# The first modulation stage: weight blocks stationary, conditioning columns moving

## The chip, the core and the metric

The kernel is one program on one core of a Trainium2 chip. The core has a matrix engine (TensorE; PE for its matmuls, PEld for the loads of the operand that stays in the array), a vector engine (DVE), a scalar engine (ACT), a general engine (POOL), and a queue from which nearly all transfers are issued (SP). Each engine takes its instructions in order; they meet through semaphores. The metric is device time in microseconds of one execution, and each kernel is run several times.

A matmul has two operands. The stationary one is loaded into the array first, in an instruction of its own, and then the columns of the moving one are streamed past it. A matmul of 32-bit floats is executed as two passes, so that each matmul of the program shows in the trace as two loads and two matmuls. Where the program splits a number itself into a high and a low part ("fp32r"), one pass is made for each.

## What is computed

One layer of a diffusion backbone on 1024 latent tokens and 256 context tokens, with a model width of 1024. What matters here is its first step: both conditioning vectors go through one matrix, and the first two of the six results modulate the normalised inputs.

```python
m_lat = (jax.nn.silu(c) @ w_mod[l] + b_mod[l]).reshape(B_, 1, N_MOD, D)
m_ctx = (jax.nn.silu(c_ctx) @ w_mod[l] + b_mod[l]).reshape(N_MOD, D)
h_lat = rms_norm(x, norm_mix[l]) * (1.0 + m_lat[:, :, 1]) + m_lat[:, :, 0]
h_ctx = rms_norm(ctx, norm_mix[l]) * (1.0 + m_ctx[1]) + m_ctx[0]
...
ccq, ccf, ccb, cci, ... = features(h_ctx, w_in[l], ...)
aq, ak, av, bq, bk, bv, cq, cf, cb, ci, cg, gates = features(h_lat, w_in[l], ...)
```

After it come the projections of the context tokens, the projections of the latent tokens, a recurrence, two attentions, a merge, and a gated feed-forward part, which fill the rest of the time.

## The kernel before

Channels lie on the 128 partitions, in KT = 8 blocks of 128. The host lays out the part of the matrix that the first step needs as eight blocks `w_mod01[i]` of 1 MB: 128 partitions (input channel within its block) by 2 results (shift and scale, index j) by 8 input blocks (k) by 128 output channels. `scc` holds the two activated conditioning vectors, 128 by 8 by 2.

The stage is the loop `for i in range(KT)` near the start of `build`. It runs on four engines, and for PE its order is the order of the code (`manual_schedule`); on the other engines and the SP queue a scheduler orders the instructions, and every transfer waits until the transfer eight before it has landed. For six of the eight blocks the two columns `scc[:, k]` are the stationary operand and the weights stream: eight matmuls of 256 columns into `pr`, two rows of results. ACT copies the two rows out (`row`), and two small transposes per block (`mod_row`, into `pm`) bring the channels back onto the partitions; the transposes of a block stand in the PE queue behind the matmuls of the next one. The other two blocks (1 and 4, `MOD_OFF`) are worked off by DVE in 16 operations each into `acc`, and PE transposes the sums (`pt`), which DVE adds up. `mod_done` adds the bias and makes the scale `a01`.

Along the way come the norm of the context (`ctx_norm`: a square on ACT, a sum on DVE, two transposes `rcc` on PE, a power on POOL, two transposes `rpc`), and for each finished block `ctx_h`: a product on DVE (`cx`) and a bias on ACT, which make the block k of the context's input `ch`. The constants of the recurrence (`lower_bounds`, tile `lbs`) and three weight blocks for the context projections (`w_raw`) are loaded between the weight blocks.

Behind the stage two generators are woven together: `ctx_all`, the projections of the context (PE matmuls `czf`, `czb`, `czv` for four heads, then `ckv`), and `lat_norm`, which squares the latent tokens on ACT (`sqx` from `xn`), turns their norm on PE (`rpx`), and makes the latent tokens' input `hh`, `hl` with `finish_h`. When both are done the first projection of the latent tokens, `zq`, begins.

Of the kernel before, what the change touches and what calls it, by code (L numbers as in the profile page):

```python
# [9 lines left out]
F32 = mybir.dt.float32  # L10
# [3 lines left out]
ALU = mybir.AluOpType  # L14
AX = mybir.AxisListType
# [3 lines left out]
P = 128  # L19
D = 1024  # L20
KT = D // P
# [22 lines left out]
WPRIO_C = 30  # L44
WM = 8
WPRIO_D = 30
WAT = 5
MPRIO = 100
CXAT = 1
LBAT = 3  # L50
NORMAT = 3

MOD_OFF = (1, 4)
MOD_FIN = {3: (1,), 6: (4,)}
CTX_K = (0, 2, 1, 3, 5, 4, 6, 7)

NPOOL = 6
# [13 lines left out]
U_C = {"q": 0, "f": 4, "b": 8, "v": 12, "g": 16, "gate": 20}  # L71
# [20 lines left out]
def build(tc, ins, out, dbg=None):  # L92
    nc = tc.nc
    V, A, G, T, SP = nc.vector, nc.scalar, nc.gpsimd, nc.tensor, nc.sync
    with ExitStack() as top:
# [12 lines left out]
        def ct(shape, name, dt=F32):  # L108
            return const.tile(shape, dt, tag=name, name=name)

        def cs(shape, name, dt=F32):
            return small.tile(shape, dt, tag=name, name=name)
# [7 lines left out]
        def bank(tag, name, shape=(P, 4, P), dt=F32):  # L120
            return ps.tile(list(shape), dt, tag=tag, name=name)
# [12 lines left out]
        scc = cs([P, KT, 2], "scc")  # L134
# [5 lines left out]
        ident = ct([P, P], "ident")  # L140
# [40 lines left out]
        def w_raw(src, nk, ncol):  # L181

            tag, bufs = (("wr", WR), ("wh", WH), ("wl", WL))[cnt[0] % 3]
            cnt[0] += 1
            with tc.high_priority(offset=wprio[0]):
                raw = wp.tile([P, 1024], F32, tag=tag, name=f"{tag}{cnt[0]}", bufs=bufs)
                SP.dma_start(raw, src)
            return raw.rearrange("p (k n) -> p k n", k=nk)
# [24 lines left out]
        def lower_bounds():  # L213

            SP.dma_start(lbr, ins["lb"])
            V.tensor_tensor(out=lt, in0=lbr, in1=lbr, op=ALU.subtract)
            A.activation(lt, lt, AF.Exp)
            V.reciprocal(lb, lt)
            V.tensor_tensor(out=lt, in0=lt, in1=lb, op=ALU.mult)
            V.tensor_tensor(out=lt, in0=lt, in1=lt, op=ALU.subtract)  # L220
            V.tensor_scalar(out=lb, in0=lt, scalar1=0.0, scalar2=1.0, op0=ALU.max, op1=ALU.min)
            V.tensor_scalar(out=oml, in0=lb, scalar1=-1.0, scalar2=1.0, op0=ALU.mult, op1=ALU.add)
# [40 lines left out]
        def rms_bc(r, n, name, tag):  # L263
            nt = n // P
            if n > 512:
                rp = mm2(f"rp{name}").rearrange("p a b -> p (a b)")
            else:
                rp = bank(tag, f"rp{name}", (P, n))
            for t in range(nt):
                T.transpose(rp[:, t * P:(t + 1) * P], r[:, t:t + 1].to_broadcast([P, P]), ident)  # L270
            return rp[:, :n]
# [7 lines left out]
        with ExitStack() as s0:  # L279
# [7 lines left out]
            xm_ = Aligned(xw.enter_context(tc.tile_pool(name="xm_", bufs=1)))  # L287

            units0 = []
            accs = {}  # L290
            pend = []
            rows = []

            def mod_done(i, pm):

                V.tensor_tensor(out=m01[:, i], in0=pm, op=ALU.add,
                                in1=bmod[:, i:i + KT + 1:KT][:, :, None].to_broadcast([P, 2, 2]))
                V.scalar_tensor_tensor(out=a01[:, i], in0=m01[:, i, 1], scalar=1.0,
                                       in1=gains[:, 0, i:i + 1].to_broadcast([P, 2]), op0=ALU.add, op1=ALU.mult)
                pend.append(i)  # L300

            def mod_row(i, row):
                pm = bank("a", f"pm{i}", (P, 2, 2))
                for j in range(2):
                    T.transpose(pm[:, j], row[:, j], ident[0:2, 0:2])
                mod_done(i, pm)

            def ctx_norm():
                csq = xm_.tile([P, KT, LC], F32, tag="csq", name="csq")
                A.activation(csq, cx, AF.Square)  # L310
                css = xm_.tile([P, LC], F32, tag="css", name="css")
                V.reduce_sum(out=css, in_=csq.rearrange("p k t -> p t k"), axis=AX.X)
                return rms_r(xm_, [css], LC, "c", False)

            def ctx_h():
                while pend:
                    k = pend.pop(0)
                    V.scalar_tensor_tensor(out=cx[:, k], in0=cx[:, k], scalar=a01[:, k, 1:2], in1=rc,
                                           op0=ALU.mult, op1=ALU.mult)
                    A.activation(ch[:, k], cx[:, k], AF.Identity, bias=m01[:, k, 0, 1:2])  # L320

            mo = ExitStack()
            mo.enter_context(tc.manual_schedule(engines={mybir.EngineType.PE}))
            for i in range(KT):
                wm = xm_.tile([P, 2, KT, P], F32, tag="wm", name=f"wm{i}", bufs=WM)
                SP.dma_start(wm, ins["w_mod01"][i].rearrange("p (j k c) -> p j k c", j=2, k=KT))
                if i == LBAT:
                    lower_bounds()
                if i == CXAT:
                    SP.dma_start(cx, ins["ctxT"].rearrange("(k p) t -> p k t", p=P))  # L330
                if WAT <= i < WAT + 3:
                    units0.append(w_raw(ins["w_cm"][U_C["fbv"[i - WAT]]], KT, P))
                if i in MOD_OFF:
                    acc = accs[i] = xm_.tile([P, 2, 2, P], F32, tag="acc", name=f"acc{i}", bufs=2)
                    for k in range(KT):
                        for v in range(2):
                            if k == 0:
                                V.tensor_scalar(out=acc[:, v], in0=wm[:, :, k], scalar1=scc[:, k, v:v + 1], scalar2=None,
                                                op0=ALU.mult)
                            else:  # L340
                                V.scalar_tensor_tensor(out=acc[:, v], in0=wm[:, :, k], scalar=scc[:, k, v:v + 1],
                                                       in1=acc[:, v], op0=ALU.mult, op1=ALU.add)
                    continue
                pr = bank("b", f"pr{i}", (P, 2, P))
                with tc.high_priority(offset=MPRIO):
                    for k in range(KT):
                        T.matmul(pr[0:2], scc[:, k], wm[:, :, k], start=k == 0, stop=k == KT - 1)
                    row = xm_.tile([2, 2, P], F32, tag="row", name=f"row{i}", bufs=3)
                    A.copy(row, pr[0:2])
                rows.append((i, row))  # L350
                if len(rows) > 1:
                    mod_row(*rows.pop(0))
                if i == KT - 1:
                    mod_row(*rows.pop(0))
                for n in MOD_FIN.get(i, ()):
                    pm = xm_.tile([P, 2, 2], F32, tag="pm", name=f"pm{n}")
                    pt = bank("b", f"pt{n}", (P, 2, 2, P))
                    for v in range(2):
                        for j in range(2):
                            T.transpose(pt[:, j, v], accs[n][:, v, j], ident)  # L360
                    V.reduce_sum(out=pm, in_=pt, axis=AX.X)
                    mod_done(n, pm)
                if i == NORMAT:
                    rc = ctx_norm()
                if i == NORMAT + 2:
                    rc = rms_bc(rc, LC, "c", "b")
                if i >= NORMAT + 2:
                    ctx_h()
# [125 lines left out]
            for h in range(CH):  # L494
                pt = bank("a", f"ckp{h}", (P, 2, 2, P))
# [75 lines left out]
        with ExitStack() as sp3:  # L571
# [5 lines left out]
            for nm, g in (("A", None), ("q", qnb), ("k", knb)):  # L577
                tb = p3.tile([P, LT, 2, 2, 32], F32, tag=f"tb{nm}", name=f"tb{nm}", bufs=1)
                for r in range(2):
                    if g is None:  # L580
                        G.tensor_copy(tb[:, :, :, r], cs)
                    else:
                        G.tensor_tensor(out=tb[:, :, :, r], in0=cs,
                                        in1=g[:, None, None, r * 32:(r + 1) * 32].to_broadcast([P, LT, 2, 32]),
# [199 lines left out]
        for k in range(KQ):  # L784
            h1, h2 = xm[k], xm[k + KQ]
            b = {nm: [p[:, k] for p in blk[nm]] for nm in ("T1", "T2", "T3")}
# [171 lines left out]
        for tb in range(2):  # L958
            xt = p2.tile([P, KT, LH], F32, tag="xt", name=f"xt{tb}", bufs=2)
            ss = []  # L960
            for mh in range(2):
# [7 lines left out]
                for f2_ in range(FT // 2):  # L969
                    w = w_unit(ins["w_down"][mh * (FT // 2) + f2_], 2, 512)  # L970
                    for f1 in range(2):
                        f = f2_ * 2 + f1
# [21 lines left out]
        for i in range(4, KT):  # L994
            z0 = 0
            for n in LAST if i == KT - 1 else (LH,):
                z = (bank("b", f"dl{i}{z0}", (P, LH)) if (i + (z0 > 0)) % 2 else mm2(f"dl{i}{z0}")[:, 0])[:, :n]
                for f0 in range(0, FT, 8):
                    nk = min(8, FT - f0)
                    w = w_unit(ins["w_dlast"][i - 4][:, f0 * P:(f0 + nk) * P], nk, P)  # L1000
                    for k in range(nk):
                        f = f0 + k
# [574 lines left out]
```

## Time and profile before

| | |
|---|---|
| time, median of 3 runs | 2128.88 us |
| lowest and highest | 2126.53 and 2129.55 us |
| span of the profiled execution, first to last instruction | 2127.9 us |
| PE busy | 2085.8 us, 98% |
| DVE busy | 1380.5 us, 65% |
| ACT busy | 1001.2 us, 47% |
| POOL busy | 288.1 us, 14% |
| transfers, mean over the span | 108 GB/s |

The profiled execution's time is known as its span; no other time is listed for it. It lies 1.0 us below the median and inside the range of the runs.

In a row of the timeline stand the start of an instruction or of a run of alike ones, how long it lasted, the engine, the line of the program, the operation, and out<-in with the shapes; "x16" is the number of instructions in the run; in brackets stand the idle time of the engine before it and what ended that. A shape "128*2 128x256" of a matmul says that the stationary operand has 128 rows and 2 columns and that 256 columns stream. A matmul is shown with its way through the array, so that matmuls overlap in the rows; the pace is read from one start to the next. A row of windows gives for each stretch the busy time and number of instructions of each engine, the granted TensorE clock as a share of full speed, the busy share of the transfer engines, and GB/s.

### The profile page before, as it was taken

The page shows a single profiled execution, that of the slowest core. Times are in us where ns is not written, and L with a number is a line of the kernel's source. Part 1 is how long each engine was busy: PE and PEld are TensorE (multiplying, and loading weights), DVE is VectorE, ACT ScalarE, POOL GpSimd, SP SyncE. Part 2 cuts the span into 40 slices and gives each one's busy share as a digit, 9 for nine tenths or more (in the row PEclk, how much of TensorE's full clock was granted, in tenths as well). Part 3 has the DMA queues.
Part 4 walks back from the last instruction along what each step waited for, and adds up shares of the span by engine and source line. Part 5 has one row for each costly group of instructions (what it writes and reads, how often), then busy time and mean ns, then how long its engine had stood idle before and what let it go on. Part 6 is the DMA issues. An engine that isn't in the chain of part 4 may idle for free.

```text
span 2127.9 us, 30555 instructions
## 1 busy us (share of the span) xinstructions
PE 2085.8 (98%) x11686; PEld 1743.1 (82%) x11686; DVE 1380.5 (65%) x2299; ACT 1001.2 (47%) x1761; POOL 288.1 (14%) x257
## 2 busy tenths in 40 slices
PE   7999999999999999999999999999999999999997
PEld 4888888888988888878888788888888888888887
DVE  4736756636665777678887746569777777664423
ACT  4333333311123777678888734346445544453222
POOL 0000000010021222100000000011333344100111
PEclk9999999999999999999999999999999999999999
DMA  9511111136543211211100354641222222285342
GB/s 359 207 44 36 46 50 41 46 113 214 186 137 123 78 59 41 80 55 35 35 28 28 115 200 142 194 156 55 99 79 89 80 80 88 81 287 201 109 126 86
DMA packets 95490, 229.28 MB, mean 108 GB/s; under 512 B 10736, under 2 KB 35824, under 8 KB 94320
## 3 DMA queue, kind: packets, MB, share of 16 engines
q1 hardware_dynamic: 95344, 227.33, 32.1%
q8 instruction: 92, 1.51, 0.3%
q14 instruction: 54, 0.44, 0.1%
HBM read 181.68 MB, written 45.61 MB: 107 GB/s over the span
## 4 chain that ended last, share of the span: by engine, by line
PE 69%; DVE 3%; ACT 2%; issue 1%; DMA 1%; POOL 1%; SPq 0%; DVEq 0%; ACTq 0%; POOLq 0%
PE pp L1321 4%; PE gz L199 3%; PE dn L929 3%; PE dn L928 3%; PE dn L930 3%; PE gz L200 3%; PE gz L201 3%; PE up L852 2%; PE up L853 2%; PE up L854 2%; PE po L1307 2%; PE po L1308 2%; PE br L200 2%; PE br L201 2%; PE br L199 2%; PE upd L853 2%
## 5 line engine op out<-in xcount | busy, mean ns | idle before, releaser
L175 ACT CAST wh<-wr 128x1024 fp32r<-128x1024 f32 (+1 forms) x139 | 145.1, 1044 | 398.7 <-PE dn L929 69.1
L176 DVE TENSOR_TENSOR wl<-wr,wh 128x1024 fp32r<-128x1024 f32 (+1 forms) x139 | 171.1, 1232 | 221.1 <-ACT wh L175 206.7
L1326 DVE TENSOR_TENSOR pl<-pp,ph 128x512 fp32r<-128x512 f32 x236 | 159.3, 687 | 29.2 <-ACT ph L1325 23.5
L199 PE MATMUL gz<-hh,wh 128*128 128x512 f32 x384 | 156.3, 408 | 3.1 <-ACT gs L523 3.1
L1325 ACT CAST ph<-pp 128x512 fp32r<-128x512 f32 x236 | 135.7, 587 | 37.4 <-PE pp L1321 35.3
L201 PE MATMUL gz<-hh,wl 128*128 128x512 f32 x384 | 152.3, 397 | 0.0
L200 PE MATMUL gz<-hl,wh 128*128 128x512 f32 x384 | 152.1, 396 | 0.0
L210 PE MATMUL tm<-wl,hh 128*128 128x256 f32 x384 | 108.9, 283 | 3.3 <-DVE wl L176 3.3
L209 PE MATMUL tm<-wh,hh 128*128 128x256 f32 x384 | 108.9, 284 | 0.9 <-ACT qo L615 0.9
L211 PE MATMUL tm<-wh,hl 128*128 128x256 f32 x384 | 108.6, 283 | 0.0
L1307 PE MATMUL po<-ph,VHL 128*128 128x512 f32 x236 | 106.1, 450 | 1.4 <-ACT ph L1325 1.0
L929 PE MATMUL dn<-ac,wh 128*128 128x512 f32 x256 | 99.7, 390 | 0.0
L930 PE MATMUL dn<-ac,wl 128*128 128x512 f32 x256 | 99.6, 389 | 0.0
L928 PE MATMUL dn<-ac,wh 128*128 128x512 f32 x256 | 99.6, 390 | 0.0
L1308 PE MATMUL po<-pl,VHL 128*128 128x512 f32 x236 | 97.1, 411 | 0.1
L199 PEld LDWEIGHTS gz<-hh,wh 128*128 128x128 f32 x384 | 72.7, 189 | 17.2 <-ACT gs L523 5.2
L201 PEld LDWEIGHTS gz<-hh,wl 128*128 128x128 f32 x384 | 72.5, 189 | 15.0
L200 PEld LDWEIGHTS gz<-hl,wh 128*128 128x128 f32 x384 | 72.8, 190 | 11.6
L210 PEld LDWEIGHTS tm<-wl,hh 128*128 128x128 f32 x384 | 73.7, 192 | 4.3 <-DVE wl L176 4.0
L1321 PE MATMUL pp<-ident,plat 128*128 128x128 f32 x512 | 76.6, 273 | 0.0
L1321 PEld LDWEIGHTS pp<-ident,plat 128*128 128x128 f32 x512 | 62.7, 140 | 16.9 <-DVE pl L1326 1.2
L199 PE MATMUL br<-yh,wh 128*128 128x512 f32 x192 | 74.3, 390 | 1.6 <-ACT yh L1468 1.6
(1420 smaller groups left out, 5898.7 us busy)
## 6 DMA issues: line engine op xcount, KB each, us to landing
wr<-in_w_cm SPq DMA_DIRECT2D x48, 512.0 KB, 3.7
wr<-in_w_up SPq DMA_DIRECT2D x44, 512.0 KB, 3.5
wr<-in_w_down SPq DMA_DIRECT2D x33, 512.0 KB, 3.5
wmr<-in_w_mod SPq DMA_DIRECT2D x32, 512.0 KB, 4.5
gate_d<-gs SPq DMA_DIRECT2D x48, 256.0 KB, 2.3
sgt<-gate_d SPq DMA_DIRECT2D x24, 512.0 KB, 3.4
act_d<-u SPq DMA_DIRECT2D x22, 512.0 KB, 2.6
st<-act_d SPq DMA_DIRECT2D x44, 256.0 KB, 4.5
```

Source lines behind the costliest of these rows:

```text
L175: A.copy(hi[:, :n], raw[:, :n])
L176: (lo_eng or V).tensor_tensor(out=lo[:, :n], in0=raw[:, :n], in1=hi[:, :n].bitcast(F32), op=ALU.subtract)
L199: T.matmul(psl, wh[:, k, c], hh[:, k0 + k, cols], start=s, stop=False)
L200: T.matmul(psl, wh[:, k, c], hl[:, k0 + k, cols], start=False, stop=False)
L201: T.matmul(psl, wl[:, k, c], hh[:, k0 + k, cols], start=False, stop=e)
L210: T.matmul(psl, hh[:, k, toks], wl[:, k % 4, :], start=False, stop=False)
L928: T.matmul(z, w[0][:, c], h[0], start=s, stop=False)
L929: T.matmul(z, w[0][:, c], h[1], start=False, stop=False)
L930: T.matmul(z, w[1][:, c], h[0], start=False, stop=e)
L1307: T.matmul(po, vv, ph, start=n == 0, stop=False)
L1321: T.transpose(pp[:, h], PT(h, n), ident)
L1326: V.tensor_tensor(out=pl, in0=pp, in1=ph.bitcast(F32), op=ALU.subtract)
```

## The change

All eight weight blocks are now requested first, followed by the constants and the three weight blocks for the context. Then each of the eight blocks is worked off on PE alone, with the operands exchanged: a piece of 128 by 128 weights is stationary and the two columns of `scc` stream, so that the results come out with the channels on the partitions. The path over DVE, the copies of the rows and all the transposes back are gone.

```diff
-WAT = 5
-MPRIO = 100
-LBAT = 3
-MOD_OFF = (1, 4)
-MOD_FIN = {3: (1,), 6: (4,)}
...
+            def wm_load(i):
                 wm = xm_.tile([P, 2, KT, P], F32, tag="wm", name=f"wm{i}", bufs=WM)
                 SP.dma_start(wm, ins["w_mod01"][i].rearrange("p (j k c) -> p j k c", j=2, k=KT))
-                if i == LBAT:
-                    lower_bounds()
+                wms.append(wm)
+
+            for i in range(KT):
+                wm_load(i)
                 if i == CXAT:
                     SP.dma_start(cx, ins["ctxT"].rearrange("(k p) t -> p k t", p=P))
-                if WAT <= i < WAT + 3:
-                    units0.append(w_raw(ins["w_cm"][U_C["fbv"[i - WAT]]], KT, P))
-                if i in MOD_OFF:
...
+            lower_bounds()
+            for nm in "fbv":
+                units0.append(w_raw(ins["w_cm"][U_C[nm]], KT, P))
+            for i in range(KT):
+                wm = wms[i]
+                pm = bank("ab"[i % 2], f"pm{i}", (P, 2, 2))
+                for j in range(2):
                     for k in range(KT):
...
-                pr = bank("b", f"pr{i}", (P, 2, P))
-                with tc.high_priority(offset=MPRIO):
-                    for k in range(KT):
-                        T.matmul(pr[0:2], scc[:, k], wm[:, :, k], start=k == 0, stop=k == KT - 1)
-                    row = xm_.tile([2, 2, P], F32, tag="row", name=f"row{i}", bufs=3)
-                    A.copy(row, pr[0:2])
-                rows.append((i, row))
...
+                        T.matmul(pm[:, j], wm[:, j, k], scc[:, k], start=k == 0, stop=k == KT - 1)
+                mod_done(i, pm)
                 if i == NORMAT:
                     rc = ctx_norm()
```

How this moves the instructions is shown at three places. In these rows stand the line, the operation, out<-in with the number of the tile, the shape of the result, and how often the row repeats. First PE, in the stage from its third matmul group to the first context projection, before:

```order
L305 MATMUL pm_168<-ident,row_133 128x2 x2
L347 MATMUL pr_183<-wm_173,scc 2x256 x8
L305 MATMUL pm_194<-ident,row_166 128x2 x2
L360 MATMUL pt_200<-ident,acc_138 128x128 x4
L249 MATMUL rcc_213<-ident,css 128x128 x2
L347 MATMUL pr_242<-wm_238,scc 2x256 x8
L305 MATMUL pm_253<-ident,row_192 128x2 x2
L270 MATMUL rpc<-ident,rsc 128x128 x2
L347 MATMUL pr_273<-wm_269,scc 2x256 x8
```

And the same stretch now:

```order
L330 MATMUL pm_191<-scc,wm_127 128x2 x16
L330 MATMUL pm_210<-scc,wm_129 128x2 x16
L244 MATMUL rcc_234<-ident,css 128x128 x2
L330 MATMUL pm_240<-scc,wm_131 128x2 x16
L330 MATMUL pm_259<-scc,wm_133 128x2 x16
L265 MATMUL rpc<-ident,rsc 128x128 x2
L330 MATMUL pm_293<-scc,wm_135 128x2 x16
L330 MATMUL pm_314<-scc,wm_137 128x2 x16
L409 MATMUL czv_399<-wl_151,ch 128x128 x8
L401 MATMUL czf_354<-ch,wr_147 128x256 x8
```

A block is now 16 matmuls with a result of 2 columns, where it was 8 matmuls with a result of 256 columns and 2 transposes; the stage holds eight such blocks on PE, where it held six. Of the first head's `czv` half now stands ahead of its `czf`.

Second ACT, from the square of the context to the second head, before (`ch` is the context's input, `sqx` a square of latent tokens `xn`, `snegcf` and `cF` read the result of `czf`):

```order
L349 COPY row_251<-pr_242 2x256
L320 ACTIVATE ch<-cx,m_97 128x256 x4
L349 COPY row_282<-pr_273 2x256
L320 ACTIVATE ch<-cx,m_97 128x256 x2
L389 ACTIVATE sqx_367,rsx<-xn_365 128x1024
L349 COPY row_315<-pr_306 2x256
L389 ACTIVATE sqx_371,rsx<-xn_369 128x1024
L320 ACTIVATE ch<-cx,m_97 128x256 x2
L389 ACTIVATE sqx_389,rsx<-xn_387 128x1024
L1033 ACT_TABLE_LOAD
L1033 ACTIVATE snegcf_359<-czf_350 128x256
```

And now:

```order
L307 ACTIVATE ch<-cx,m_97 128x256 x7
L212 ACT_TABLE_LOAD
L212 ACTIVATE lbs<-lbs 128x8
L307 ACTIVATE ch<-cx,m_97 128x256
L358 ACTIVATE sqx_371,rsx<-xn_369 128x1024
L358 ACTIVATE sqx_375,rsx<-xn_373 128x1024
L1002 ACT_TABLE_LOAD
L1002 ACTIVATE snegcf_363<-czf_354 128x256
```

The copies of rows are gone; the first two squares of latent tokens have moved behind the last block of `ch`, and the third behind the first head's `czf`.

Third ACT again, further on, at the second head's projections, where the squares end. Before:

```order
L389 ACTIVATE sqx_439,rsx<-xn_437 128x1024
L1033 ACTIVATE snegcf_432<-czf_423 128x256
L1034 ACTIVATE cF<-czf_423 128x256
L389 ACTIVATE sqx_443,rsx<-xn_441 128x1024
L1033 ACTIVATE snegcb_456<-czb_447 128x256
L1034 ACTIVATE cF<-czb_447 128x256
```

And now:

```order
L1002 ACTIVATE snegcf_436<-czf_427 128x256
L1003 ACTIVATE cF<-czf_427 128x256
L358 ACTIVATE sqx_443,rsx<-xn_441 128x1024
L1002 ACTIVATE snegcb_460<-czb_451 128x256
L1003 ACTIVATE cF<-czb_451 128x256
L358 ACTIVATE sqx_447,rsx<-xn_445 128x1024
L410 COPY cV<-czv_482 128x2x128
```

The eighth and last square stood ahead of the two operations that read the second `czb` and stands behind them now. On PE the eight transposes `rpx` that need all the squares stood ahead of the second head's `czv`; now 13 of the 16 matmuls of that `czv` stand ahead of them. A few operations behind the start of `zq` the queues have the same order again in both kernels, to the end.

More of the change, by code (lines that the diff above doesn't have):

```diff
@@ L289, in build @@
             units0 = []
-            accs = {}
             pend = []
-            rows = []
             def mod_done(i, pm):
@@ L300, in mod_done @@
                 pend.append(i)
[L302 to L306, printed above, removed]
             def ctx_norm():
@@ L323, in build @@
             mo.enter_context(tc.manual_schedule(engines={mybir.EngineType.PE}))
-            for i in range(KT):
+            wms = []
+            def wm_load(i):
                 wm = xm_.tile([P, 2, KT, P], F32, tag="wm", name=f"wm{i}", bufs=WM)
                 SP.dma_start(wm, ins["w_mod01"][i].rearrange("p (j k c) -> p j k c", j=2, k=KT))
-                if i == LBAT:
-                    lower_bounds()
+                wms.append(wm)
+            for i in range(KT):
+                wm_load(i)
@@ L329, in build @@
                 if i == CXAT:
                     SP.dma_start(cx, ins["ctxT"].rearrange("(k p) t -> p k t", p=P))
-                if WAT <= i < WAT + 3:
-                    units0.append(w_raw(ins["w_cm"][U_C["fbv"[i - WAT]]], KT, P))
-                if i in MOD_OFF:
-                    acc = accs[i] = xm_.tile([P, 2, 2, P], F32, tag="acc", name=f"acc{i}", bufs=2)
-                    for k in range(KT):
[L336 to L343, printed above, removed]
@@ L344, in build @@
-                pr = bank("b", f"pr{i}", (P, 2, P))
-                with tc.high_priority(offset=MPRIO):
-                    for k in range(KT):
-                        T.matmul(pr[0:2], scc[:, k], wm[:, :, k], start=k == 0, stop=k == KT - 1)
-                    row = xm_.tile([2, 2, P], F32, tag="row", name=f"row{i}", bufs=3)
-                    A.copy(row, pr[0:2])
-                rows.append((i, row))
[L351 to L362, printed above, removed]
+            lower_bounds()
+            for nm in "fbv":
+                units0.append(w_raw(ins["w_cm"][U_C[nm]], KT, P))
```

## The prediction

> **What bounds the kernel now.** I read the page first, then the windows of the stage, then the timeline.
>
> ```profile
> PE 2085.8 (98%) x11686; PEld 1743.1 (82%) x11686; DVE 1380.5 (65%) x2299; ACT 1001.2 (47%) x1761; POOL 288.1 (14%) x257
> ```
>
> PE is busy for 98% of the span, so a time that the first stage adds to PE's queue is carried to the end unless PE waits for something later that absorbs it. The question is how long PE needs until the first context projection, and what it meets behind it.
>
> ```profile
> 30.00:40.00 10.00, 8.63 (x44) 4.58 (x42) 4.18 (x14) 5.93 (x14) 0.00 (x0) 1.00 1.04 408
> ...
> 7.80 5.44 PE L347 MATMUL pr<-wm,scc 128*2 128x256 f32 x16 [7.80 <-DMA wm<-in_w_mod]
> 15.68 3.62 PE L347 MATMUL pr<-wm,scc 128*2 128x256 f32 x16 [2.44 <-DMA wm<-in_w_mod]
> 23.68 0.38 PE L249 MATMUL rcc<-ident,css 128*128 128x128 f32 x2
> 27.75 0.43 PE L270 MATMUL rpc<-ident,rsc 128*128 128x128 f32 x2
> 33.67 3.62 PE L347 MATMUL pr<-wm,scc 128*2 128x256 f32 x16 [0.78 <-DVE pm L361]
> 37.80 0.28 PE L305 MATMUL pm<-ident,row 2*128 2x2 f32 x2 [0.29 <-ACT row L349]
> 38.01 3.72 PE L432 MATMUL czf<-ch,wr 128*128 128x256 f32 x16
> 45.02 3.73 PE L440 MATMUL czv<-wl,ch 128*128 128x128 f32 x32
> 48.59 3.62 PE L432 MATMUL czf<-ch,wr 128*128 128x256 f32 x16
> 55.92 1.09 PE L270 MATMUL rpx<-ident,rsx 128*128 128x128 f32 x8 [0.26 <-POOL rsx L260]
> 60.42 3.62 PE L432 MATMUL czf<-ch,wr 128*128 128x256 f32 x16
> 95.00 0.58 PE L199 MATMUL zq<-hh,wh 128*128 128x512 f32 x1
> ```
>
> The transfers run at about 410 GB/s, so a block, 128 by 2048 floats or 1.05 MB, takes 2.6 us. The third block ends PE's wait at 15.68; the last, five blocks later, is there at about 28.5 when nothing stands between (15.68 + 5 × 2.6). A block needs 3.62 us on PE. Hence PE leaves the stage at 38.0 because of its own matmuls, of the wait of 2.44 us, and of short waits; from 38.0 to 95.0 it waits only the 0.26 us before `rpx`.
>
> **What a block costs after the change.** It becomes 32 pairs of a load of 128 columns and a matmul that streams two. No row shows such pairs in a long run. The nearest are the `czv` pairs, whose loads are the same and whose matmuls stream 128 columns:
>
> ```profile
> 44.80 3.76 PEld L440 LDWEIGHTS czv<-wl,ch 128*128 128x128 f32 x32
> ...
> L440 PEld LDWEIGHTS czv<-wl,ch x128: 190/192/192, 44.8 to 81.2; 128*128 128x128 f32 x128
> ...
> L347 PEld LDWEIGHTS pr<-wm,scc x96: 80/85/127, 7.8 to 36.7; 128*2 128x2 f32 x96
> ...
> 19.22 0.20 PEld L305 LDWEIGHTS pm<-ident,row 2*128 2x128 f32 x2 [0.44 <-issue]
> ```
>
> From 45.02 to 48.59 there are 32 pairs, 0.1116 us each, while a load lasts 0.192: loads overlap with what runs. A load of two columns lasts 0.085, so 126 more columns cost 0.107. Load and stream both need about 0.107 there, and the stream is all that shrinks. At full clock a pair is therefore bounded by 0.107 below and 0.192 above (no overlap at all); I take 0.1116, a block of 3.57 us. That is no faster than the 3.62 us of now, and there are eight instead of six: the change removes 12 small transposes, 8 of `acc`, the copies and the waits, and adds two blocks.
>
> The Trainium skill, page "TensorE: Matmul & The Clock Gate", Part 3, says that a weight load overlaps with a running matmul only where their row groups differ. By that the full 0.192 would stand in each pair, and the time would be that of the second rival; the `czv` rows, 128 rows in every load and yet 0.1116 us apart, speak against it, and the row decides.
>
> **The clock.** This is what I think decides the case.
>
> ```profile
> 9.04 0.13 PEld L347 LDWEIGHTS pr<-wm,scc 128*2 128x2 f32 x1 [0.30 <-issue]
> 9.46 0.13 PEld L347 LDWEIGHTS pr<-wm,scc 128*2 128x2 f32 x1 [0.30 <-issue]
> ...
> 11.50:15.00 3.50, 1.74 (x8) 0.51 (x6) 3.50 (x10) 1.73 (x2) 0.00 (x0) 1.00 1.06 410
> 594.00:598.00 4.00, 1.77 (x12) 1.30 (x10) 3.31 (x9) 1.34 (x3) 1.54 (x1) 1.00 0.60 175
> 598.00:602.00 4.00, 4.00 (x11) 3.15 (x12) 0.06 (x1) 0.00 (x0) 0.00 (x0) 0.58 0.63 218
> ...
> 597.98 0.50 PE L199 MATMUL gz<-hh,wh 128*128 128x512 f32 x1 [2.23 <-ACT gs L523]
> ...
> 599.34 0.33 PEld L201 LDWEIGHTS gz<-hh,wl 128*128 128x128 f32 x1
> 599.77 0.33 PEld L199 LDWEIGHTS gz<-hh,wh 128*128 128x128 f32 x1
> ```
>
> The first block's pairs are 0.42 us apart until about 11.5, and 0.226 in later blocks (3.62 / 16): TensorE starts at half clock, though the clock column, which has no record that early, prints 1.00. It is released after 3.7 us of matmuls. At 597.98 PE had waited 2.23 us, and right after that the clock fell to half for some 3.4 us. So the clock follows how much PE did in the last microseconds: 44% busy (1.77 of 4.0) was followed by half clock (0.58 on the mean of the next 4 us), 50% (1.74 of 3.5) was not. What counts as doing is not shown directly. Two columns of 128 in the array were enough at the start, so it isn't the filled part of the array; in every released stretch columns streamed for a large part of the time. In the changed stage they stream for 2 of every 128 column times, under 2%. If streaming counts, the clock stays at half through the whole stage. If loads count too, or any instruction in the array, it is released at 11.5 as now. At half clock loads stretch as well: 0.33 us instead of 0.19. With 0.127 for two columns at half clock (the longest of the `pr` loads), 126 more cost 0.203, so a pair takes at least 0.206 and at most twice 0.1116, 0.223; I take 0.214.
>
> The Trainium skill, same page, Part 1, has half clock as the state of rest and a window of about 3.4 us; its Part 4 says that transposes do not count as busy in the same way as other matmuls. The trace agrees on the window; whether transposes or loads count, no run here shows. By loads not counting, the time is that of the forecast; by loads counting, that of the first rival.
>
> **The sum.** Start at 7.80, when the first block is there. 8 × 32 pairs at 0.214 are 54.8 us (52.7 to 57.1). `rcc` and `rpc` cost 0.4 each at full clock and I take 1.0 for both. The first context matmul starts at 63.6 instead of 38.0: **+25.6**. Transfers don't matter in it, all blocks being there by 28.5. Then the clock needs up to 3.4 us of real matmuls to be released, which costs half of that at most; I take **+1.5** (0.6 to 1.9).
>
> Behind the stage stand these rows:
>
> ```profile
> 34.98 1.04 ACT L389 ACTIVATE sqx<-xn 128x1024 f32<-128x1024 f32 x1
> 52.79 1.06 ACT L389 ACTIVATE sqx<-xn 128x1024 f32<-128x1024 f32 x1
> 53.74 0.20 ACT L389 ACTIVATION_READ_ACCUMULATOR sqx<-xn 128x1 f32 x1
> 55.70 0.38 ACT L1033 ACTIVATE snegcb<-czb 128x256 f32<-128x256 f32 x1 [1.76 <-PE czb L432]
> 55.98 0.38 ACT L1034 ACTIVATE cF<-czb 128x256 f32<-128x256 f32 x1
> ...
> 36.14 3.01 SPq L387 DMA_DIRECT2D xn<-in_x  x2
> 46.36 1.07 SPq L187 DMA_DIRECT2D wr<-in_w_cm  x1
> ...
> wr<-in_w_cm SPq DMA_DIRECT2D x5, 512.0 KB, 11.0
> ...
> 38.33 0.15 DVE L296 TENSOR_TENSOR m<-pm,bmod 128x4 f32<-128x4 f32 x1
> 38.71 0.48 DVE L318 SCALAR_TENSOR_TENSOR cx<-cx,a,rpc 128x256 f32<-128x256 f32 x1
> ...
> 38.70 1.03 ACT L320 ACTIVATE ch<-cx,m 128x256 f32<-128x256 f32 x2
> 85.72 1.22 DVE L176 TENSOR_TENSOR wl<-wr,wh 128x1024 fp32r<-128x1024 f32 x1
> ```
>
> The last square ended at 53.94 and `rpx` began 2.0 us later. Now that square stands behind `snegcb` and `cF`. `czb` ends about 0.2 before `snegcb`; from there 0.2 + 0.67 for these two + 1.25 for the square + 2.0 to `rpx` are 4.1 us, and PE meanwhile has 13/16 of a `czv`, 2.9 us. PE waits 1.2 us where it waited 0.26: **+1.0**. The total is 25.6 + 1.5 + 1.0 = 28.1 us. On the profiled execution's span of 2127.9, which is its time as far as it is known and 1.0 below the median, that is **2156 us**.
>
> What costs nothing, and under what cover: DVE loses 28 + 4 operations and ACT six copies; PE waited for DVE 0.78 us before 33.67 and for ACT 0.29 at the end, and both are in the 38.0. The constants `lbs` now come behind the last block; the recurrence's DVE work reads them only behind `czf`, microseconds later. From the last block's result to its `ch` passes 1.7 us (38.0 to 39.7: two small operations, 0.48 on DVE, 0.5 on ACT), and the `czv` half ahead needs that block last, after 15/16 of 3.4 us at half clock, so PE doesn't wait; at full clock, after 1.6, it waits 0.2. On SP the fifth `xn` waits for the first square, which has moved from 34.98 to behind the last `ch`; behind that `xn` in SP's queue stand the other latent tokens and the weight blocks from the second head's `czv` on. They start 30 us later while PE is 27 later. The nearest is `wr` of the third head, issued at 46.36 and read by `czf` at 60.42; with the median of 11.0 us to landing it has 3 us to spare. The transfer engines will have been idle by then, so I take 0; without that cover it costs up to 3. DVE's long run from `rpx` to `zq`'s weights (85.72 + 1.22) moves with `rpx` and leaves 8 us before PE's 95.0.
>
> **The rivals.** (1) Full clock. 17 pairs at half clock to 11.5, 239 at 0.1116 to 38.2, `rcc` and `rpc` to 39.0: +1.0, +0.2 for `ch`, +1.0 for `rpx`: 2130, no measurable change (a measurement of this kernel can tell 0.2%, 4.3 us, from nothing). For it: PE's instruction rows would be close to gapless, and if these count, the release at 11.5 is repeated. Against it: no released stretch in this trace has so little streaming.
> (2) Loads that don't hide. At full clock 7 of the 8 blocks cost 32 × 0.192 = 6.1, the first 2 more, in all 51 us, so the stage ends at about 59.8: +21.8 + 1.0, 2151. With half clock as well, 0.33 a pair: 84.5 + 8.8, an end at 93, +55, 2186. Against both stand the `czv` rows.
> (3) The other side: faster. The loads of `pm` by `row`, 128 columns of two partitions, follow each other 0.065 us apart (two in 0.20). If the new loads did that, a block would take 2.1 us, less than its landing, and PE would leave at 28.5 + 2.1 = 31, then wait for the `czv` weights that now land second behind all blocks: 6 us gained, 2122. It decides if a pair falls under 0.095 (eight blocks of 3.0 us). Against it: these are transposes of two rows, and the load rows give 0.107 for full columns.
> That the change doesn't do what it says I exclude: PE's order shows the 16 matmuls a block.
>
> **How the numbers follow.** Half clock through the stage 0.54, full clock 0.33, unhidden loads at full clock 0.05 and at half clock 0.04, faster loads 0.04. The forecast's own range is 2152 to 2161 (pairs −2.1 to +2.3, release −0.9 to +0.4, `wr` up to +3). Rival 1 spans 2128 to 2134, where its pairs reach 0.12. Both are needed for 8 in 10, so the range goes from 2128 to 2161. Slower: 0.54 + 0.09 = 0.63; the same: 0.32, nearly all of rival 1; faster: 0.05, the last case and the rest of rival 1.
>
> **What would show it.** The clock column of the windows from 8 to 63: 0.50 in the forecast, 1.00 from 11.5 in rival 1, or pairs of 0.21 against 0.11 us where the column has no record. The first `czv` at 63.6 against 39. A wait of PE for POOL before `rpx` of 1.2. Loads of 0.33 us that start 0.21 apart mean overlap at half clock; loads of 0.19 that start 0.19 apart mean rival 2. I'm wrong if the clock is released in the stage, or if the weights of the third head come late by more than 3 us.

## The result and the profile after

| | before | changed |
|---|---|---|
| median of 4 runs each, one chip, us | 2127.70 (2126.43 to 2129.55) | 2157.72 (2156.51 to 2158.61) |
| ratio, with its 95% interval | | 1.0138 (1.0123 to 1.0152) |
| profiled execution: span, us | 2127.9 | 2155.9 (its time 2157.71) |

The changed kernel is slower by 30.0 us on the medians; the spans of the two profiles differ by 28.0. A span is some 2 us shorter than the time of its run (2155.9 against 2157.71), so each is compared with its like. The engines' shares say almost nothing of that. This is the first line of the page of the changed kernel, with busy us, share of the span and instructions of each engine:

```profile
PE 2118.9 (98%) x11826; PEld 1791.5 (83%) x11826; DVE 1368.3 (63%) x2265; ACT 998.7 (46%) x1755; POOL 288.3 (13%) x257
```

PE is as full as before, with 33 us more in it. Where they lie is seen in the timeline of the changed kernel, PE's rows from the start to `zq` (start and duration in us, operation, shape, count, and the idle time ahead with what ended it):

```profile
7.66 27.44 PE L330 MATMUL pm<-scc,wm 128*128 128x2 f32 x128 [7.66 <-DMA wm<-in_w_mod]
34.96 0.67 PE L244 MATMUL rcc<-ident,css 128*128 128x128 f32 x2
35.42 13.65 PE L330 MATMUL pm<-scc,wm 128*128 128x2 f32 x64
...
49.40 13.65 PE L330 MATMUL pm<-scc,wm 128*128 128x2 f32 x64
62.91 3.76 PE L409 MATMUL czv<-wl,ch 128*128 128x128 f32 x16
66.46 3.99 PE L401 MATMUL czf<-ch,wr 128*128 128x256 f32 x16
70.29 3.62 PE L401 MATMUL czb<-ch,wh 128*128 128x256 f32 x16
...
86.31 1.09 PE L265 MATMUL rpx<-ident,rsx 128*128 128x128 f32 x8 [0.81 <-POOL rsx L255]
...
94.81 3.73 PE L409 MATMUL czv<-wl,ch 128*128 128x128 f32 x32
98.97 3.72 PE L401 MATMUL czf<-ch,wr 128*128 128x256 f32 x16 [0.42 <-ACT cF L1003]
103.32 3.72 PE L401 MATMUL czb<-ch,wh 128*128 128x256 f32 x16 [0.64 <-ACT cF L1003]
...
119.09 1.89 PE L423 MATMUL ckv<-wr,ch 128*128 128x256 f32 x8
122.95 1.99 PE L423 MATMUL ckv<-wl,ch 128*128 128x256 f32 x8 [1.98 <-ACT ckvs L427]
...
126.33 0.58 PE L194 MATMUL zq<-hh,wh 128*128 128x512 f32 x1
```

Once the first block is there, the stage has no gap: 128 pairs in the 27.3 us from 7.66 to 34.96 are 0.2133 us each, up to the last one. Sixteen `czv` pairs still take 3.55 us (62.91 to 66.46), 0.222 each, and only the `czb` at 70.29 has its normal duration. The weight loads of the stage tell the same. This is the tile view of `pm` in the changed kernel (shortest, median and longest ns of a load), and behind it a row of the windows (length; busy us of PE, PEld, DVE, ACT, POOL; granted clock; DMA share; GB/s):

```profile
L330 PEld LDWEIGHTS pm<-scc,wm x256: 288/333/338, 7.6 to 62.6; 128*128 128x128 f32 x128
...
8.00:30.00 22.00, 22.00 (x105) 22.00 (x105) 4.50 (x7) 1.91 (x1) 0.00 (x0) 1.00 1.02 410
```

The median load lasts 333 ns, the half-clock duration, yet the clock column prints 1.00. As at the start of the kernel before, it prints that until the clock's first change, and until then the durations have to be read in its place. PE and its load queue are each shown busy for 22.00 of 22 us, and the clock is still not released.

### The profile page after: what moved, and what is told of

Its sections match the earlier page's. It is cut to its first block, busy times and chain, and to the rows that moved or that the text cites. A ratio compares the mean times of both kernels' runs of the same rounds, so it can differ in the third digit from the quotient of the medians.

```text
span 2155.9 us, 30790 instructions
## 1 busy us (share of the span) xinstructions
PE 2118.9 (98%) x11826; PEld 1791.5 (83%) x11826; DVE 1368.3 (63%) x2265; ACT 998.7 (46%) x1755; POOL 288.3 (13%) x257
## 4 chain that ended last, share of the span: by engine, by line
PE 68%; DVE 3%; ACT 2%; issue 1%; POOL 1%; DMA 1%; SPq 0%; DVEq 0%; ACTq 0%; POOLq 0%
PE pp L1290 4%; PE gz L194 3%; PE dn L898 3%; PE dn L897 3%; PE gz L195 3%; PE dn L899 3%; PE gz L196 3%; PE up L821 2%; PE up L822 2%; PE up L823 2%; PE po L1276 2%; PE po L1277 2%; PE br L195 2%; PE br L196 2%; PE br L194 2%; PE upd L822 2%
## 5 line engine op out<-in xcount | busy, mean ns | idle before, releaser
L1295 DVE TENSOR_TENSOR pl<-pp,ph 128x512 fp32r<-128x512 f32 x236 | 159.4, 688 | 29.7 <-ACT ph L1294 24.1
L195 PEld LDWEIGHTS gz<-hl,wh 128*128 128x128 f32 x384 | 72.7, 189 | 11.6
L195 PE MATMUL br<-yl,wh 128*128 128x512 f32 x192 | 75.0, 392 | 0.3 <-DVE yl L1438 0.3
```

The costliest lines, as they stand in the source:

```text
L195: T.matmul(psl, wh[:, k, c], hl[:, k0 + k, cols], start=False, stop=False)
L1295: V.tensor_tensor(out=pl, in0=pp, in1=ph.bitcast(F32), op=ALU.subtract)
```

## The experiments

The question was whether the stage is slow because of the clock, or because such pairs take 0.21 us by themselves. Four kernels ran first. `wide64` streams the two columns 64 times each, so that a pair streams as many columns as its load has; `wide32` and `wide16` do it 32 and 16 times, 64 and 32 columns. Only the first copy is used afterwards. The edit on the changed kernel, here of `wide64` (the others have 32 and 16 in place of 64):

```diff
-                pm = bank("ab"[i % 2], f"pm{i}", (P, 2, 2))
+                pm = bank("ab"[i % 2], f"pm{i}", (P, 2, 2, 64))
...
-                        T.matmul(pm[:, j], wm[:, j, k], scc[:, k], start=k == 0, stop=k == KT - 1)
-                mod_done(i, pm)
+                        T.matmul(pm[:, j], wm[:, j, k], scc[:, k, :, None].to_broadcast([P, 2, 64]),
+                                 start=k == 0, stop=k == KT - 1)
+                mod_done(i, pm[:, :, :, 0])
```

> The changed kernel, with each of the two conditioning columns streamed 64 times (128 moving columns in place of 2; the copies are ignored, the result is the same). Theory A (the clock follows streaming): pairs are at half clock to about 11.5 us and then 0.11 us apart, the first context matmul starts at 39 instead of 63, the time is 2129 to 2133 us. Rival B (pairs of a full weight load and a short matmul cost 0.21 us by themselves, by loads that do not hide): pairs stay 0.21 us or more apart, 2156 us or more.

> As before with 32 copies of each column, 64 moving columns, half of the time that a load needs. Theory A: about 50% streaming lies above the share at which the clock fell in the first profile (44% busy), so it is released in the stage: 2129 to 2134 us. Rival B: 2156 us.

> As before with 16 copies, 32 moving columns, a quarter of the time of a load. Theory A: 25% streaming lies under the share that was followed by half clock, so the clock stays at half through the stage: 2155 to 2159 us, as with two columns. If any streaming beyond a few per cent released it: 2130 us. Rival B: 2156 us.

| columns per pair | kernel | us (before, same chip) | load, median ns | first context matmul at |
|---|---|---|---|---|
| 128 | `wide64`, 10 runs | 2127.96 (2128.32) | 191 | 39.27 |
| 64 | `wide32`, one run | 2158.26 (2128.32) | 333 | 62.91 |
| 32 | `wide16`, one run | 2158.46 (2128.32) | 333 | 62.89 |
| 2 | the changed kernel | 2157.72 (2127.70) | 333 | 62.91 |

The ratio of `wide64` is 1.0000 (0.9990 to 1.0009). These are its rows from the timeline and the tile view:

```profile
7.70 17.00 PE L330 MATMUL pm<-scc,wm 128*128 128x128 f32 x128 [7.70 <-DMA wm<-in_w_mod]
24.54 0.38 PE L244 MATMUL rcc<-ident,css 128*128 128x128 f32 x2
24.76 7.31 PE L330 MATMUL pm<-scc,wm 128*128 128x128 f32 x64
31.91 0.38 PE L265 MATMUL rpc<-ident,rsc 128*128 128x128 f32 x2
...
39.27 0.61 PE L410 MATMUL czv<-wl,ch 128*128 128x128 f32 x4
...
L330 PEld LDWEIGHTS pm<-scc,wm x256: 189/191/333, 7.7 to 39.1; 128*128 128x128 f32 x128
```

With the same loads and 64 times the streamed columns, the loss is gone. From 24.76 to `rpc` at 31.91, 64 pairs take 7.15 us, 0.1117 each. So a pair does not need 0.21 us, and loads of 191 ns that start 112 ns apart do overlap. And what releases the clock is streamed columns: 128 a pair do it, 64 a pair do not in 55 us. `wide32` came out against its expectation, which was that half of the columns would release the clock.

One thing qualifies `wide64`. Behind its stage the order is not quite that of the changed kernel: 4 pairs of `czv` stand ahead of the first `czf` instead of 16, and three waits of PE for ACT that are told below are absent. `wide48`, below, keeps both.

The Trainium skill, page "TensorE: Matmul & The Clock Gate", Part 1, lets the clock follow how busy PE has been, over a window of about 3.4 us. Measured here, "busy" cannot be read as the busy share of PE, nor of its loads: both were 100% for 55 us at half clock.

The next kernel asks whether loads at least hold a clock that has been released. `warm` runs six wide matmuls of ones, whose result is unused, mostly while the first block is still on its way, and then the changed stage with two columns:

```diff
+WUP = 6
...
+            hot = xm_.tile([P, 512], F32, tag="hot", name="hot")
+            V.memset(hot, 1.0)
+            wu = bank("a", "wu", (P, 512))
+            for n in range(WUP):
+                T.matmul(wu[0:2], ones[:, 0:2], hot, start=n == 0, stop=n == WUP - 1)
```

> The changed kernel with two moving columns, and six matmuls of 512 moving columns of ones ahead of the stage, before the first weight block is there; their result is not used. Theory A: the clock is released near 5 us, the first block runs at 0.11 us a pair, then the clock falls back within two windows of 3.4 us and the rest is at half clock: 2153 to 2157 us. Rival C (loads hold a clock that was released, they only cannot release it): the whole stage at 0.11 us a pair, 2128 to 2132 us. Rival B: pairs of 0.21 us throughout, 2157 us.

It took 2155.03 us in one run (before 2128.32). From its timeline and its windows, and last the rows with which two stretches of its timeline begin that both end at 13.5:

```profile
1.50 6.90 PE L317 MATMUL wu<-hot,ones 128*2 128x512 f32 x12 [1.50 <-DVE hot L314]
8.33 24.56 PE L336 MATMUL pm<-scc,wm 128*128 128x2 f32 x128
...
5.00:11.50 6.50, 6.50 (x37) 3.69 (x35) 0.00 (x0) 0.00 (x0) 0.00 (x0) 1.00 1.01 401
11.50:30.00 18.50, 18.50 (x90) 18.50 (x89) 4.50 (x7) 1.91 (x1) 0.00 (x0) 0.50 1.02 415
...
8.46 5.23 PE L336 MATMUL pm<-scc,wm 128*128 128x2 f32 x37
11.36 2.32 PE L336 MATMUL pm<-scc,wm 128*128 128x2 f32 x11
```

Here the clock has a record, as it was released once: 1.00 up to 11.5, then 0.50, with PE and its loads busy for all of the 18.5 us. Gapless loads neither release the clock nor hold it. The last two rows give the pace of two-column pairs at full clock: 37 − 11 = 26 pairs from 8.46 to 11.36, 0.1115 us each. That is the pace of the 128-column pairs in `wide64`, so repeating the columns costs nothing beside the load, and the clock alone makes 0.2133 of it.

The next kernels bracket the share of streaming: `wide48` (96 columns, as above) and `warm32` (64 columns behind the warm-up of `warm`). With them ran `order_only`, the order of the loads alone, and `mix64`, of which below.

> The changed kernel with 96 moving columns (48 copies each), three quarters of the time of a load. 64 columns left the clock at half, 128 released it. Theory A, if the share of streaming is what counts and the bound lies below 75%: released in the first block, 2127 to 2132 us; if above: 2156 to 2159 us. This run places the bound.

> 64 moving columns as in the run that stayed at half clock, and the six streaming matmuls of ones ahead of the stage, which released the clock at 4.7 us in the run with 2 columns. Theory A1 (one bound, above 50%, for release and for hold): the clock falls back in the stage as it did there, 2154 to 2157 us. Theory A2 (holding needs less than releasing, as the 43 to 50% busy stretches of the first profile that kept full clock suggest): full clock to the end of the stage, 2125 to 2130 us.

`wide48` took 2128.74 us (before 2127.94) and `warm32` 2130.55, one run each. `warm16` has 32 columns behind the warm-up:

> 32 moving columns and the six streaming matmuls of ones ahead of the stage. With 2 columns the released clock fell back after 6.8 us, with 64 it was held. Theory A2, with a hold bound in the region where the first profile kept and lost the clock (30 to 45% of streaming): 29% falls back, 2154 to 2157 us. If holding needs less than 29%: 2126 to 2131 us. This run narrows the bound.

It took 2149.88 us in one run (before 2128.68), 4 us under the range for a clock that falls back. Its `zq` starts at 123.76, 2.6 us ahead of that of the changed kernel; the other 5 us lie behind `zq` and were not traced. First the loads of `wide48`, then the windows of `warm32`, then those of `warm16`:

```profile
L330 PEld LDWEIGHTS pm<-scc,wm x256: 190/192/338, 7.9 to 39.4; 128*128 128x128 f32 x128
...
7.00:20.00 13.00, 13.00 (x103) 11.10 (x101) 3.68 (x5) 1.91 (x1) 0.00 (x0) 1.00 1.03 410
20.00:38.00 18.00, 18.00 (x165) 18.00 (x164) 5.48 (x21) 4.50 (x9) 0.72 (x1) 1.00 1.02 410
```

```profile
8.20:11.60 3.40, 3.40 (x24) 2.43 (x23) 0.00 (x0) 0.00 (x0) 0.00 (x0) 1.00 1.02 380
11.60:15.00 3.40, 3.40 (x26) 3.40 (x25) 0.32 (x2) 1.64 (x1) 0.00 (x0) 0.77 1.08 415
15.00:18.40 3.40, 3.40 (x18) 3.40 (x17) 0.00 (x0) 0.27 (x1) 0.00 (x0) 0.50 1.02 424
```

The same 64 columns a pair that do not release the clock in `wide32` hold it from 7 to 38 us in `warm32`. The two kernels differ by the warm-up alone, and by 27.7 us. With 32 columns the clock is lost: a mean of 0.77 from 11.6 to 15.0 is full clock up to about 13.4, some 4 us behind the warm-up's end. So, for pairs like these, the share that releases lies between 64 and 96 of 128 columns, and the share that holds between 32 and 64: there are two bounds, and they differ. Each is placed by single runs.

Then the order of the loads. `order_only` is the kernel before with all block loads, the lower bounds and the first head's weights queued ahead of the work; `exch_only` (the second diff) is the opposite, the exchange of operands for all eight blocks with the load order of before:

```diff
+            wms = []
             for i in range(KT):
...
+                wms.append(wm)
...
+            lower_bounds()
+            for nm in "fbv":
+                units0.append(w_raw(ins["w_cm"][U_C[nm]], KT, P))
+            for i in range(KT):
+                wm = wms[i]
```

```diff
-MOD_OFF = (1, 4)
-MOD_FIN = {3: (1,), 6: (4,)}
+MOD_OFF = ()
+MOD_FIN = {}
...
-                pr = bank("b", f"pr{i}", (P, 2, P))
...
+                pm = bank("ab"[i % 2], f"pm{i}", (P, 2, 2))
...
+                        T.matmul(pm[:, j], wm[:, j, k], scc[:, k],
...
+                mod_done(i, pm)
```

> The kernel before with only the second half of the change: all eight weight blocks are requested first, then the constants and the three context weight blocks; the matmuls, the DVE blocks and the transposes stay as they were. Theory A (the operands' exchange, through the clock, is the whole loss): 2126 to 2131 us, no measurable change. Rival D (the order of the loads, by the squares and the later weights, carries part of the loss): more than 2133 us.

> The other half of the change alone: the kernel before with its load order (constants and context weights between the weight blocks), but all eight blocks on PE with the weights stationary and two moving columns, nothing on DVE and no transposes. Theory A: half clock from 7.8 us to the first context matmuls, which start near 63; 2154 to 2160 us, the whole loss of the change. Rival D (the load order carries part of it): under 2150 us.

`order_only` took 2129.65 us in 10 runs, ratio 1.0007 (0.9998 to 1.0017): by itself the order costs nothing that can be told from noise, and at most 3.6 us. Its profile has its first context matmul 2.2 us later than the kernel before, and this has a place, in its timeline and windows:

```profile
34.17 5.30 PE L350 MATMUL pr<-wm,scc 128*2 128x256 f32 x16 [1.23 <-DVE pm L364]
40.19 3.72 PE L435 MATMUL czf<-ch,wr 128*128 128x256 f32 x16
...
31.60:35.00 3.40, 1.78 (x11) 0.95 (x11) 2.83 (x12) 1.13 (x4) 0.00 (x0) 1.00 1.01 400
35.00:38.40 3.40, 3.40 (x9) 0.97 (x8) 0.02 (x1) 1.55 (x3) 0.00 (x0) 0.51 1.02 408
```

Its last block meets 3.4 us at half clock, right behind 3.4 us in which PE was busy for 1.78, and takes 5.30 instead of 3.62 us. Here 52% busy (1.78 of 3.4) were followed by half clock, where 50% (1.74 of 3.5) were not in the kernel before. So the busy share of PE, from which the expectation of `wide32` was worked out, gives no bound.

`exch_only` gave 2151.93 us in one run, 2 us under what was expected of it. A single run can't settle 2 us, so it was repeated with four runs, beside the changed kernel on the same chip:

> The exchange of the operands alone, timed again in rounds beside the changed kernel on the same chip; its single look gave 2151.9. If the load order is worth nothing, it comes out with the changed kernel within 2 us; if the order that the loads and the squares take behind the stage is worth what the traces show at the turned norm (2 us), it lies 1 to 4 us below it: 2152 to 2156.

> The changed kernel itself, as the yardstick on the same chip: 2156 to 2159 us.

The exchange alone took 2153.65 us (2153.34 to 2154.92), ratio 1.0126 (1.0109 to 1.0143), and the whole change 2157.05 (2155.14 to 2157.74), ratio 1.0139 (1.0123 to 1.0154), against 2127.38 before. The exchange is 26.3 of the 29.7 us. The 1.7 of `order_only` do not explain the other 3.4, since the changed kernel has no gap at that place. The trace of `exch_only` shows what it is spared:

```profile
63.39 5.62 PE L427 MATMUL czf<-ch,wr 128*128 128x256 f32 x16 [0.30 <-issue]
...
98.33 3.62 PE L427 MATMUL czf<-ch,wr 128*128 128x256 f32 x16
101.78 3.62 PE L427 MATMUL czb<-ch,wh 128*128 128x256 f32 x16
...
122.43 0.59 PE L199 MATMUL zq<-hh,wh 128*128 128x512 f32 x1
```

Its stage ends no earlier (63.39 against 62.91), but the three waits for ACT at 98.97, 103.32 and 122.95 are absent, and `zq` starts at 122.43 instead of 126.33. `order_only` is spared them too: from its first context matmul to `zq` (40.19 to 97.18) it takes 56.99 us, exactly as the kernel before.

Last, a kernel built on this: `mix64` is the kernel before with its load order and its two blocks on DVE, and its other six blocks keep the weights stationary with 128 moving columns, which saves the copies of rows and their transposes. The edit is that of `exch_only` without its first four lines, and with the copies of `wide64`.

> A version meant to beat both: the kernel before with its load order and its two blocks on DVE, and the other six blocks with the weights stationary and 128 moving columns, so that the row copies and small transposes go. Theory A: clock released at 11.5 us, PE leaves the stage at about 36 instead of 38, 2125 to 2129 us. If weights stationary cost in themselves (rival B): slower than 2132.

It took 2124.69 us in 11 runs, ratio 0.9988 (0.9979 to 0.9997): 0.12% under the kernel before, and the interval just excludes no change. Three rows of its timeline:

```profile
37.48 0.61 PE L435 MATMUL czv<-wl,ch 128*128 128x128 f32 x4
37.92 3.69 PE L427 MATMUL czf<-ch,wr 128*128 128x256 f32 x16
...
94.44 0.58 PE L199 MATMUL zq<-hh,wh 128*128 128x512 f32 x1
```

PE leaves the stage 0.5 us earlier (37.48 against 38.01), not the 2 that were expected, and `zq` starts 0.56 earlier (95.00 before). The median fell by 3.25 us; the rest arises later in the span and was not traced to a cause. It stays open.

## Why the prediction was right

The forecast was 28.1 us on the span; it was 28.0, and 30.0 on the medians. The mechanism was right. That the sum came out within 0.1 us was luck: terms that were off cancel. By its own steps:

| step | forecast | measured |
|---|---|---|
| pairs at half clock; first context matmul | +25.6 | 62.91 − 38.01 = +24.9 |
| release of the clock behind the stage | +1.5 (0.6 to 1.9) | +2.15 |
| wait before `rpx` | +1.0 | 0.81 − 0.26 = +0.55 |
| ACT late for the fourth head's `czf` and `czb` and for `ckv` | not foreseen | 0.59 + 0.90 + 2.13 = +3.62 |
| to `zq`, all in all | +28.1 | 126.33 − 95.00 = +31.3 |
| from `zq` to the end | 0 | −3.3 |

**The clock.** The step that decided the case, that loads don't count and columns do, held, and `wide64` and `warm` show it from both sides. Rival 1 (full clock) lacked its premise, that PE's rows count. Rival 2 (loads that don't hide) would have left `wide64` slow as well. Rival 3 (pairs under 0.095) is out by the 0.1115 of two-column pairs at full clock in `warm`. The pair was 0.2133 against the 0.214 taken, and `rcc` and `rpc` cost 0.46 us each (34.96 to 35.42), near the 1.0 for both.

**The release was taken too small.** The half `czv` took 3.55 us instead of 1.78 (16 pairs of 0.1116), and the `czf` behind it 3.83 instead of 3.45 (62.91 to 66.46 to 70.29, each start to start). That is 1.77 + 0.38 = 2.15, just past the upper end of 1.9. At half clock half of the time is lost, so the clock came some 4.3 us behind the stage, where the forecast allowed 3.4 at most.

**What the sum lacked** are ACT's three late results. From one start to the next the three places take 4.16, 4.35 and 3.86 us instead of 3.57, 3.45 and 1.73. That is 3.62 of the 31.3 at `zq` (the waits in brackets, 3.04, leave out the time in which the matmuls ahead run out), and with it the rows add up to all but 0.1. The forecast followed ACT's queue as far as `rpx` and no further. These rows of ACT's timeline in the changed kernel show what stood in it:

```profile
97.22 1.15 ACT L271 ACTIVATE hh<-x,m 128x1024 fp32r<-128x1024 f32 x1 [1.24 <-DVE x L270]
98.28 0.36 ACT L1002 ACTIVATE snegcf<-czf 128x256 f32<-128x256 f32 x1
...
121.59 1.04 ACT L170 CAST wh<-wr 128x1024 fp32r<-128x1024 f32 x1 [7.11 <-DMA wr<-in_w_cm]
122.54 0.37 ACT L427 COPY ckvs<-ckv 128x256 f32<-128x256 f32 x1
```

What stands ahead in ACT's queue goes first, ready or not. The fifth of the eight `hh` of the latent tokens, itself waiting for DVE, stands ahead of the `snegcf` and `cF` that read the third head's `czf`, and PE's next `czf` waits for that `cF`. The sixth does the same to the third head's `czb`. And a cast of `zq`'s weights, which waits 7.11 us for its transfer, stands ahead of the copy `ckvs` that PE waits 1.98 us for. The other traces narrow the cause. `exch_only` has only the exchange and `order_only` only the order of the loads, and neither has these waits. Of the kernels with both, `wide16`, `wide32`, `wide48` and the three `warm` ones have all of them, at half and at full clock (1.7 to 2.0 us at `ckv`), but `wide64` has none. In `wide64` and `exch_only` four `hh` stand ahead of that `snegcf` instead of five, and the second `ckvs` stands ahead of the cast. So the waits hang on the order in which ACT's queue comes out, not on the clock; what makes the scheduler choose it was not separated.

**What came back later.** The waits of PE between 470 and 700 us, first of the kernel before, then of the changed one (engine, what waited, for whom: us in total, times, longest):

```profile
PE tm L210 <- DVE wl L176: 3.3, 2, 2.0
PE gz L199 <- ACT gs L523: 2.6, 2, 2.2
PE tm L209 <- ACT qo L615: 0.9, 1, 0.9
```

```profile
PE gz L194 <- ACT gs L492: 2.5, 2, 2.1
PE tm L205 <- DVE wl L171: 2.4, 2, 1.4
```

Here 6.8 us of waits became 4.9. A PE that comes later waits less for engines whose work has moved less than its own; that this is the reason was not tested. Some 2 us of the 3.3 are seen in this stretch; the rest is spread thin. Nor are the 3.3 firm: over all profiles of these kernels the part from `zq` to the end takes between 2024.3 us (`warm16`) and 2032.9 (the kernel before), and 2029.6 in the changed kernel. On the medians, which differ by 30.0, only 1.3 of the 31.3 would have come back.

**What was right at nothing:** the third head's `wr`, for which up to 3 us were held ready, did not make PE wait, and neither did `ch`.

**Small slips in the working.** The last square takes 1.15 us in its row (52.79 to 53.94), not 1.25. The terms of the range give 2153 as its lower end, not 2152. And that 44% busy lost the clock and 50% kept it is no bound, as `order_only` shows. None of them moves the forecast by more than 0.1 us.

## What to carry to other kernels

Keeping the weights stationary and streaming only a few columns kept TensorE at half clock here, however densely PE was filled: what counted was streamed columns, not loads. Where the weights must be stationary, stream about as many columns as the load has, by repeating them if need be; beside a load of 128 columns that took no time here, and was worth some 30 us in a stage of 31. And after a change that moves one engine by tens of microseconds, follow the other engines' strict queues up to the first point at which the order is the old one again: three waits for ACT, 3.6 us, lay just behind the place where the forecast stopped looking.

## What the runs showed of the chip that was not expected

- The clock has two bounds, not one. Starting from half clock, 64 streamed columns per load of 128 didn't release it in 55 us (`wide32`), and 96 did (`wide48`). From full clock, the same 64 held it to the end of the stage (`warm32`), and 32 lost it some 4 us behind the warm-up (`warm16`).
- This kernel can therefore be 28 us faster or slower by what ran in the 8 us ahead of one stage: `warm32` (2130.55) and `wide32` (2158.26) differ by six matmuls whose result nobody reads.
- Loads and two-column matmuls that fill PE's rows for 100% of the time reach neither bound (`warm`: clock 0.50 with PE and PEld at 18.50 of 18.50 us).
- Before the first change of the clock the profile's clock column prints 1.00, also where the kernel runs at half clock (the changed kernel from 8 to 30 us). The durations of the loads (333 against 191 ns) tell it.
